# Thirty weight tiles get their rests from an accumulating load instead of a VectorE subtraction

## The chip, the cores and the metric

The kernel runs on one core of a Trainium2 chip. The metric is the device time of one execution in microseconds (us), from its start to its end. Lower is better.

## The reference

One layer of a hybrid streaming encoder runs on 512 prompt frames and 32 sample frames. The kernel holds both as T = 544 columns. Cut to what matters here:

```python
h = rmsnorm(x, p['norm_mix'])
proj = h @ p['w_in']
z, xbc, dt_raw, hq, hf, hi, hgate, rgate, rx, mg = jnp.split(proj, split_pts, axis=-1)
...  # three token mixers: Mamba-2 SSD -> y_mb, HGRN2 -> y_hg, RG-LRU -> y_rg
branches = jnp.stack([y_mb, y_hg, y_rg], axis=0)
pb = jnp.einsum('kblc,kcd->kbld', branches, p['w_branch'])
gates = jax.nn.sigmoid(mg.reshape(b, L, N_BRANCH, D_MODEL))
merged = jnp.einsum('kbld,blkd->bld', pb, gates)
x = x + merged @ p['w_out']
...  # SwiGLU FFN, final norm
```

HGRN2 uses four of these projections: hq (its query), hf (its forget gate), hi (its value) and hgate (its output gate), for eight heads of 128 channels each.

## The kernel before

**Tiles and products.** All weights lie in DRAM as 98 groups, one array per group of 128 partitions x 8 K-blocks x 256 columns (1024 KB; a few are smaller). A group gives two *tiles* of 128 output channels. One tile is one `Step`: its weights (128 x 1024 values per tile) against 544 columns of a right-hand side. The product of two float32 numbers is made of three products of rounded numbers (float32r): each weight w is split into a rounded half `wh` and the rest `wl` = w - wh, each right-hand side into hi and lo, and TensorE computes wh*hi, wh*lo and wl*hi. `products` (L321 ff., matmuls at L338) therefore issues 32 matmuls with `wh` and then 16 with `wl`, each of 128x272. HGRN2's heaviest projections (hq2, hi, hgt) run as `Pair` instead: two tiles in seven products of quarter size (matmuls at L347), whose weights `prep_pair` makes.

**The weights' two ways.** `load_raw` (L264, queue SP) brings a group to a `raw` buffer, of which there are two. `prep` makes `wh` and `wl` of one tile, for which there are three buffers each:

- the ordinary way: ScalarE copies the tile's columns to `wh` (L319), and VectorE subtracts, wl = raw - wh (L320). The tile's columns are 8 pieces of 128 in `raw`.
- the accumulating way, so far for `fi` groups only: ScalarE copies to `wh` (L314), ScalarE writes -wh to `wl` (L315), and GpSimd issues a DMA that reads the tile's weights again from DRAM and adds them to `wl` (L316). For this the group lies by tile in DRAM: a tile's 1024 values per partition are one piece. `lay_out` reorders those groups (named in `SEVEN`) on the host. `prep_pair` uses accumulating DMAs as well (L283, 512 KB; L286, 256 KB).

**What sets the order.** `run_program` walks a list of steps. Before a step's matmuls it emits the `prep` of the step after it and, as far as two raw buffers go, the loads. Between the matmuls of a step, `advance` runs pieces of *sides*: generators with the small work of the token mixers. A scheduler then orders each engine's instructions by priority and by its own estimate of when they are ready. On the chip, each engine executes its list in order and waits at an instruction whose semaphores are not there yet.

**The place of the change.** After the SSD phase come the early HGRN2 steps: four ordinary tiles (hq0, hq1), then nine pairs, whose results go to DRAM (`kept_hq`, `kept_hi`, `kept_hgt`, L1035 and L1044). Then the HGRN2 phase proper opens (`hg_open`, a new buffer pool) with this list, each name being two tiles unless a number of tiles stands beside it:

hf0, br0 (4 tiles), hf1, br0 (4 tiles), hf2, mg1 (2 tiles), hf3, hq3, mg1 (6 tiles), then br1 (8 tiles).

After each hf, `hg_heads` (L1089) loads q, v and gate of two heads from DRAM, and two sides `hg_side` begin: transposes of v (`tok_major`, L1117 to L1121), decays on VectorE (L1141 to L1219), small matmuls (L1159 to L1211), state and output (L1224 to L1264). In these, GpSimd clears and fills `at` (L1125, L1201) and takes the power -0.5 of the output's mean square (`oss`, L1254). Names in the profile: `acc` is a tile's PSUM accumulator, `mx` a PSUM buffer of a side, `hhi`/`hlo` and `yr` are right-hand sides, `gth` a gate, `hq` (a buffer's name) holds q, v or gate of a head, `qv` a head's scaled queries, `on` a head's normed output, `rs_mb` SSD norms, `kept_mg` gates kept in DRAM.

Of the kernel before, what the change touches and what calls it, by code (L numbers as in the profile page):

```python
# [49 lines left out]
B11, B21, B22, T1, T2, T3, T4 = range(7)  # L50

EARLY = ("hq2", "hi0", "hi1", "hi2", "hi3", "hgt0", "hgt1", "hgt2", "hgt3")
SEVEN = EARLY + tuple(f"fi{m}" for m in range(22))


# [41 lines left out]
WG = {k: (i, v[0][2] // P) for i, (k, v) in enumerate(GROUPS.items())}  # L97
# [23 lines left out]
def hybrid_layer(ctx: ExitStack, tc: _tile.TileContext, a: dict, outs: list):  # L121
# [146 lines left out]
    def quarters(t):  # L268
        return t.rearrange("p k n -> p (k n)").rearrange("p (q n) -> p q n", n=512)

    def prep_pair(st):

        r = quarters(raws[st.raw])
        src = wp[WG[st.raw][0]].rearrange("p (q n) -> p q n", n=512)
        tiles = []
        for i in range(4):
            pool = wpool if i % 2 else phase["p"]
            tiles.append([pool.tile([P, NK, P], R, tag=t, name=t, bufs=3) for t in ("wh", "wl")])
        (ah, al), (bh, bl), (dh, dl), (ch, cl) = [[t.rearrange("p (q k) n -> p q (k n)", q=2) for t in x] for x in tiles]
        sa, sc = ([pt_([P, 2, T], "sums", 3)[:, :, :512] for _ in range(2)])  # L280
        S.activation(bh, r[:, 0:2], AF.Copy)  # L281
        S.activation(bl, bh.bitcast(F), AF.Copy, scale=-1.0)  # L282
        G.dma_start(bl, src[:, 0:2], accum_op=ALU.add)  # L283
        S.activation(dh[:, 0], r[:, 3], AF.Copy)
        S.activation(dl[:, 0], dh[:, 0].bitcast(F), AF.Copy, scale=-1.0)  # L285
        G.dma_start(dl[:, 0], src[:, 3], accum_op=ALU.add)  # L286
        V.tensor_tensor(sa[:, 0], r[:, 0], r[:, 2], ALU.add)
        V.tensor_tensor(sa[:, 1], sa[:, 0], r[:, 3], ALU.add)
        S.activation(ah, sa, AF.Copy)
        V.tensor_tensor(sc[:, 0], r[:, 2], r[:, 3], ALU.add)  # L290
        V.tensor_tensor(sc[:, 1], sa[:, 1], r[:, 1], ALU.add)
        V.tensor_tensor(al, sa, ah.bitcast(F), ALU.subtract)  # L292
        S.activation(ch, sc, AF.Copy)  # L293
        V.tensor_tensor(cl, sc, ch.bitcast(F), ALU.subtract)
        q = lambda x, y, i: (x[:, i].rearrange("p (k n) -> p k n", n=P), y[:, i].rearrange("p (k n) -> p k n", n=P))
        st.wts = {"s3": q(ah, al, 0), "s2": q(ah, al, 1), "a11": q(bh, bl, 0), "a12": q(bh, bl, 1), "a22": q(dh, dl, 0),
                  "s1": q(ch, cl, 0), "s4": q(ch, cl, 1)}

    def prep(st):
        if isinstance(st, Pair):  # L300
            return prep_pair(st)
        if st.wh is not None:
            return
        if st.share:
            st.wh, st.wl = st.share.wh, st.share.wl
            return
        r = raws[st.raw]
        st.wh = wpool.tile([P, NK, P], R, tag="wh", name="wh")
        st.wl = wpool.tile([P, NK, P], R, tag="wl", name="wl")
        if st.raw.startswith("fi"):  # L310
            i = st.col // P
            src = quarters(r)[:, 2 * i : 2 * i + 2]
            wh, wl = (t.rearrange("p (a k) n -> p a (k n)", a=2) for t in (st.wh, st.wl))
            S.activation(wh, src, AF.Copy)  # L314
            S.activation(wl, wh.bitcast(F), AF.Copy, scale=-1.0)  # L315
            G.dma_start(wl, wp[WG[st.raw][0]].rearrange("p (q n) -> p q n", n=512)[:, 2 * i : 2 * i + 2], accum_op=ALU.add)  # L316
            return
        src = r[:, : st.nk, st.col : st.col + P]
        S.activation(st.wh[:, : st.nk, :], src, AF.Copy)  # L319
        V.tensor_tensor(st.wl[:, : st.nk, :], src, st.wh[:, : st.nk, :].bitcast(F), ALU.subtract)  # L320
# [60 lines left out]
    def run_program():  # L381
# [9 lines left out]
        for s in program:  # L391
            if not isinstance(s, (Step, Pair)):
                s()
                continue
            while prepped < min(len(order), done + 2):
                st = order[prepped]
                while loaded < min(len(keys), pos[st.raw] + RAWB):
                    if keys[loaded] not in raws:
                        load_raw(keys[loaded])
                    loaded += 1  # L400
                prep(st)
                prepped += 1
            if isinstance(s, Pair):
                pair_products(s)
            else:
                products(s)
            if isinstance(s, Step) and s.last and s.evac:
                with tc.high_priority(offset=400):
                    s.evac(accs[s.acc])
            done += 1  # L410
            advance(BUDGET[0] / TILE_PARTS)
# [135 lines left out]
    def head():  # L547
# [54 lines left out]
        square(NK - 1)  # L602
        st = Step("rg0", 0, NK, None, "rg0")
        prep(st)
        acc3 = [mx(), mx()]
        hd["rb"] = rb = pt_([P, T], "rbx")
# [18 lines left out]
        rg_gl[0] = g  # L625
        derived()
        prep(first[0])
        rg_load()

# [421 lines left out]
    program.append(drain)  # L1051
    for key in EARLY:
        kind, pr = key[:-1], int(key[-1])
# [287 lines left out]
    for m in range(8):  # L1341
        key = f"wo{m//2}"
# [228 lines left out]
def lay_out(v):  # L1571

    cm = lambda x: x.reshape(-1, P).T
    dcol = np.repeat(v["mb_d"][0], 64)
    rows = lambda x: np.broadcast_to(x.reshape(1, -1), (P, x.size))
    src = {
        "mcw": cm(v["mb_conv_w"]), "mcb": cm(v["mb_conv_b"]), "nw": cm(v["mb_norm_w"]), "ba": cm(v["rg_b_a"]), "bi": cm(v["rg_b_i"]),
        "hgw": cm(v["hg_norm_w"]), "nm": cm(v["norm_mix"]), "lb": cm(v["hg_lb_logits"]), "rcw": cm(v["rg_conv_w"]), "rcb": cm(v["rg_conv_b"]),
        "lam": cm(v["rg_lambda"]), "nf": cm(v["norm_ffn"]), "h0": cm(v["state_rglru"]), "rch": cm(v["state_rglru_conv"]),
        "sch": cm(v["state_ssm_conv"]), "dcol": cm(dcol), "dtb": rows(v["mb_dt_bias"]), "alog": rows(v["mb_a_log"]),  # L1580
    }
    mats = {"w_in": v["w_in"][0], "w_out": v["w_out"][0], "w_ffn_in": v["w_ffn_in"][0], "w_ffn_out": v["w_ffn_out"][0]}
    mats |= {f"w_branch{b}": v["w_branch"][0, b] for b in range(3)}
    weights = np.zeros((len(GROUPS), P, NK, 256), v["w_in"].dtype)
    for i, parts in enumerate(GROUPS.values()):
        c = 0
        for name, r0, nr, c0, ncol in parts:
            weights[i, :, : nr // P, c : c + ncol] = mats[name][r0 : r0 + nr, c0 : c0 + ncol].reshape(nr // P, P, ncol).transpose(1, 0, 2)
            c += ncol
    for key in SEVEN:  # L1590
        i = WG[key][0]
        weights[i] = weights[i].reshape(P, NK, 2, P).transpose(0, 2, 1, 3).reshape(P, NK, 256)
    gates = np.zeros((P, 2, 8, P), v["rg_w_a"].dtype)
    for i, name in enumerate(("rg_w_a", "rg_w_i")):
        w = v[name][0].reshape(8, 2, 64, 64).transpose(1, 2, 0, 3)
        gates[:64, i, :, :64] = w[0]
        gates[64:, i, :, 64:] = w[1]
    r = np.arange(P)[:, None]
    c = np.arange(P)[None, :]
    consts = [c == r, r <= c, r > c, r % 32 == c[:, :32], r % 16 == c[:, :16]]  # L1600
    for h in QUADS:
        for s in range(3):
            n = (3 - s) * h
            j = r % 32
            consts.append((j // (4 * h) == c[:, : 8 * (3 - s)] // n) & (j // h % 4 == s))
    consts.append(r % 32 // 16 == 0 * c[:, :16])
    return {
        "xT": np.concatenate([v["x_prompt"][0], v["x_sample"][0]], axis=0).T,
        "params": np.concatenate([src[k] for k in PK], axis=1),
        "consts": np.concatenate(consts, axis=1).astype(np.float32),  # L1610
        "weights": weights.reshape(len(GROUPS), P, NK * 256),
        "w_dt": v["w_in"][0][:, C_DT : C_DT + 16].reshape(NK, P, 16).transpose(1, 0, 2),
        "rg_gates": gates,
        "ssm_in": v["state_ssm"][0, 0].transpose(2, 0, 1).reshape(P, 1024),
        "hg_in": v["state_hgrn"][0, 0].transpose(1, 0, 2),
        "norm_final": rows(v["norm_final"]),
    }
# [23 lines left out]
```

## Time and profile before

| | |
|---|---|
| median of 3 runs (lowest to highest) | 1347.47 us (1345.01 to 1347.68) |
| the profiled execution's own time | 1345.73 us |
| its span, first to last instruction | 1344.0 us |
| TensorE busy (PE) | 1326.4 us |
| VectorE (DVE), ScalarE (ACT), GpSimd (POOL) busy | 864.3, 643.5, 162.4 us |
| mean clock granted to TensorE | 0.997 |

PE is TensorE's matmuls and PEld its weight loads; SP issues the plain DMAs and POOL the accumulating ones. A row such as "L338 PE ... xN | busy, mean | idle <-releaser" gives a group of instructions by source line and what ended the idle time before them. A window row gives, for a stretch of time, each engine's busy time with its count of instructions, the granted clock, the busy share of the 16 DMA engines and GB/s.

### The profile page before, as it was taken

Reading aid. Unit: us, or ns where it says so; the run is one execution under the profiler, and the core shown is the slowest. Engines: PE = TensorE matmul, PEld = TensorE weight load, DVE = VectorE, ACT = ScalarE, POOL = GpSimd, SP = SyncE. Lnnn points to the kernel's source line nnn. Section 1 sums busy time; section 2 is a strip of 40 time slices with the busy share of each in tenths; the row PEclk is TensorE's granted clock in tenths of the full one; section 3 lists DMA queues with packets and bytes.
Section 4 is the critical chain, followed back from the end, with each engine's and each line's share of the span. In section 5 each row is a group of like instructions: output and inputs, shape, how many; then the busy total and the mean of one; then the engine's idle time right before and its main releaser. Section 6 shows DMA issues by size and latency. Waiting matters only on the chain. (4 is left out here: it accounts for less than half of the span.)

```text
span 1344.0 us, 26318 instructions
## 1 busy us (share of the span) xinstructions
PE 1326.4 (99%) x11034; PEld 1274.2 (95%) x11034; DVE 864.3 (64%) x1617; ACT 643.5 (48%) x1063; POOL 162.4 (12%) x263
## 2 busy tenths in 40 slices
PE   9999999999999999999999999999999999999997
PEld 9999999999998999999998888999999999999997
DVE  8887653738575677656748766455597447744753
ACT  7785744236445346553324443334666236623634
POOL 3031001011020001110111121000111011101100
PEclk9999999999999999999999999999999999999998
DMA  6212121211222348875332032622767166725621
GB/s 238 95 63 95 64 99 65 102 66 64 75 74 76 112 120 221 223 178 190 117 131 102 25 125 85 217 95 97 186 160 168 66 172 152 168 75 167 142 77 68
DMA packets 43975, 161.73 MB, mean 120 GB/s; under 512 B 5040, under 2 KB 10032, under 8 KB 31824
## 3 DMA queue, kind: packets, MB, share of 16 engines
q1 hardware_dynamic: 34496, 134.35, 28.9%
q0 software_dynamic: 8928, 25.17, 10.8%
q8 instruction: 87, 1.43, 0.4%
q10 hardware_dynamic: 432, 0.53, 0.1%
q14 instruction: 32, 0.26, 0.1%
HBM read 145.04 MB, written 14.99 MB: 119 GB/s over the span
## 5 line engine op out<-in xcount | busy, mean ns | idle before, releaser
L319 ACT ACTIVATE wh<-raw 128x1024 fp32r<-128x1024 f32 (+1 forms) x132 | 137.8, 1045 | 256.4 <-PE acc L338 218.9
L338 PE MATMUL acc<-hhi,wh 128*128 128x272 f32 x1184 | 252.6, 293 | 0.4 <-ACT cv L463 0.4
L338 PE MATMUL acc<-hlo,wh 128*128 128x272 f32 x1184 | 249.7, 290 | 0.0
L320 DVE TENSOR_TENSOR wl<-raw,wh 128x1024 fp32r<-128x1024 f32 (+1 forms) x132 | 159.0, 1204 | 81.2 <-PE acc L338 68.9
L338 PE MATMUL acc<-yr,wh 128*128 128x272 f32 x1504 | 206.3, 290 | 0.5 <-DVE gth L497 0.4
L338 PEld LDWEIGHTS acc<-yr,wh 128*128 128x128 f32 x1504 | 194.3, 188 | 2.0 <-PE acc L338 0.6
L338 PEld LDWEIGHTS acc<-hhi,wh 128*128 128x128 f32 x1184 | 186.9, 189 | 4.2 <-issue 1.3
L338 PEld LDWEIGHTS acc<-hlo,wh 128*128 128x128 f32 x1184 | 186.0, 188 | 1.6 <-issue 0.2
L338 PE MATMUL acc<-hhi,wl 128*128 128x272 f32 x1184 | 167.7, 291 | 0.0
L338 PEld LDWEIGHTS acc<-hhi,wl 128*128 128x128 f32 x1184 | 154.6, 188 | 2.6 <-issue 0.9
L347 PE MATMUL acc<-T,wh 128*128 128x272 f32 x744 | 147.2, 290 | 0.2 <-DVE pt L376 0.2
L347 PEld LDWEIGHTS acc<-T,wh 128*128 128x128 f32 x744 | 113.5, 188 | 1.5 <-DVE pt L376 0.4
L338 PE MATMUL acc<-yr,wl 128*128 128x272 f32 x752 | 106.8, 289 | 0.0
L338 PEld LDWEIGHTS acc<-yr,wl 128*128 128x128 f32 x752 | 99.0, 188 | 0.3
L347 PE MATMUL acc<-T,wl 128*128 128x272 f32 x372 | 74.2, 288 | 0.0
L347 PE MATMUL acc<-Thhi,wh 128*128 128x272 f32 x304 | 63.5, 301 | 1.0 <-ACT pt L370 0.5
L347 PE MATMUL acc<-Thlo,wh 128*128 128x272 f32 x304 | 62.8, 288 | 0.0
L347 PE MATMUL acc<-Thhi,wl 128*128 128x272 f32 x304 | 60.2, 289 | 0.2 <-DVE wl L292 0.2
L347 PEld LDWEIGHTS acc<-T,wl 128*128 128x128 f32 x372 | 57.4, 188 | 0.0
L293 ACT ACTIVATE wh<-sums 128x1024 fp32r<-128x1024 f32 x28 | 29.7, 1061 | 53.7 <-PE acc L347 49.7
L286 POOL DMA_DIRECT2D wl<-in_weights_dram x28 | 24.8, 887 | 249.7 <-ACT wl L285 217.7
L347 PEld LDWEIGHTS acc<-Thhi,wh 128*128 128x128 f32 x304 | 45.8, 188 | 5.7 <-DVE pu L361 3.1
(440 smaller groups left out, 2285.0 us busy)
## 6 DMA issues: line engine op xcount, KB each, us to landing
raw<-in_weights_dram SPq DMA_DIRECT2D x93, 1024.0 KB, 4.8
wl<-in_weights_dram POOLq DMA_DIRECT2D x34, 512.0 KB, 7.1
wl<-in_weights_dram POOLq DMA_DIRECT2D x28, 256.0 KB, 3.8
kept_mg<-gth SPq DMA_DIRECT2D x16, 272.0 KB, 2.0
gth<-kept_mg SPq DMA_DIRECT2D x16, 272.0 KB, 5.6
raw<-in_weights_dram SPq DMA_DIRECT2D x4, 768.0 KB, 4.5
xt<-in_xT_dram SPq DMA_DIRECT2D x8, 272.0 KB, 5.5
kept_hi<-pt SPq DMA_DIRECT2D x8, 272.0 KB, 3.0
```

Source lines behind the costliest of these rows:

```text
L286: G.dma_start(dl[:, 0], src[:, 3], accum_op=ALU.add)
L293: S.activation(ch, sc, AF.Copy)
L319: S.activation(st.wh[:, : st.nk, :], src, AF.Copy)
L320: V.tensor_tensor(st.wl[:, : st.nk, :], src, st.wh[:, : st.nk, :].bitcast(F), ALU.subtract)
L338: PE.matmul(acc[:, h, :HALF], l, r[:, h * HALF : (h + 1) * HALF], start=st.first and i == 0, stop=st.last and i == len(seq) - 1)
L347: PE.matmul(out, w[:, kp, :], st.rhs(n == 1, kp, j), start=start and n == 0 and kp == 0, stop=stop and n == 2 and kp == 3, skip_group_chec ...
```

## The change

The ordinary tiles of the groups hf, hq, br0 and mg1 take the accumulating way. These are 8 + 6 + 8 + 8 = 30 tiles, in 15 groups; hq2, a pair, stays as it was. The 15 groups are laid out by tile in DRAM (hq2 already was). Nothing else is edited. Line numbers behind the edit are two higher in the changed kernel (L338 becomes L340).

```diff
 EARLY = ("hq2", "hi0", "hi1", "hi2", "hi3", "hgt0", "hgt1", "hgt2", "hgt3")
+
+ADDED = ("hf", "hq", "br0", "mg1")
 SEVEN = EARLY + tuple(f"fi{m}" for m in range(22))
@@ prep
-        if st.raw.startswith("fi"):
+        if st.raw in SEVEN or st.raw.startswith(ADDED):
             i = st.col // P
             src = quarters(r)[:, 2 * i : 2 * i + 2]
             wh, wl = (t.rearrange("p (a k) n -> p a (k n)", a=2) for t in (st.wh, st.wl))
@@ lay_out
-    for key in SEVEN:
-        i = WG[key][0]
+    for key, (i, _) in WG.items():
+        if key not in SEVEN and not key.startswith(ADDED):
+            continue
         weights[i] = weights[i].reshape(P, NK, 2, P).transpose(0, 2, 1, 3).reshape(P, NK, 256)
```

The scheduler orders the changed program anew. ScalarE's list at the opening of the HGRN2 phase, before; the four copies L319 are the `wh` of hf0's second tile and of br0's tiles 0, 1 and 2, L1067 takes hf0's results out of PSUM, and L1140 is the first head's first work on q:

```order
L319 ACTIVATE wh<-raw 128x1024
L370 ACTIVATE pt<-acc 128x272
L1042 ACTIVATE pt<-pt 128x544
L319 ACTIVATE wh<-raw 128x1024
L1041 ACTIVATE pt<-pt 128x272
L319 ACTIVATE wh<-raw 128x1024
L1067 ACTIVATE hth<-acc 128x544
L319 ACTIVATE wh<-raw 128x1024
L1067 ACTIVATE hth<-acc 128x544
L1140 ACTIVATE qv<-hq 128x136x4
```

And after the change (L316 is the `wh`, L317 the new -wh):

```order
L316 ACTIVATE wh<-raw 128x1024
L372 ACTIVATE pt<-acc 128x272
L317 ACTIVATE wl<-wh 128x1024
L1044 ACTIVATE pt<-pt 128x544
L316 ACTIVATE wh<-raw 128x1024
L1043 ACTIVATE pt<-pt 128x272
L317 ACTIVATE wl<-wh 128x1024
L316 ACTIVATE wh<-raw 128x1024
L1069 ACTIVATE hth<-acc 128x544
L317 ACTIVATE wl<-wh 128x1024
L316 ACTIVATE wh<-raw 128x1024
L1069 ACTIVATE hth<-acc 128x544
```

Each -wh stands behind the PSUM read (L1043, L1069) that came next after its `wh`.

GpSimd's list from hf0 on, after the change; before, it held none of the L318 (the accumulating loads of hf0 and br0's first tile, of br0's next three, and of hf1's first), and the rest in the same order:

```order
L318 DMA wl<-in_weights_dram 128x1024 x3
L1127 MEMSET at 128x512 x2
L318 DMA wl<-in_weights_dram 128x1024 x3
L1203 COPY at<-bd 32x4x32 x4
L318 DMA wl<-in_weights_dram 128x1024
```

The loads of br0's tiles 1 to 3 now stand between the clearing of `at` and the first head's copies into it.

TensorE's list at br0's first tile, where the first head's v is transposed for the first time, before:

```order
L338 MATMUL acc<-yr,wh 128x272 x32
L338 MATMUL acc<-yr,wl 128x272 x12
L1117 MATMUL mx_7025<-cst,hq 128x128 x4
L1120 MATMUL mx<-cst,hq 32x128
L1159 MATMUL mx<-qv,hth 32x80 x16
L1160 MATMUL mx<-qv,hth 32x80
L338 MATMUL acc<-yr,wl 128x272 x4
L1117 MATMUL mx_7160<-cst,hq 128x128 x4
```

And after:

```order
L340 MATMUL acc<-yr,wh 128x272 x32
L340 MATMUL acc<-yr,wl 128x272 x8
L1119 MATMUL mx_7033<-cst,hq 128x128 x4
L1122 MATMUL mx<-cst,hq 32x128
L1161 MATMUL mx<-qv,hth 32x80 x16
L1162 MATMUL mx<-qv,hth 32x80
L340 MATMUL acc<-yr,wl 128x272 x8
L1119 MATMUL mx_7168<-cst,hq 128x128 x4
```

The transposes have moved four matmuls of the tile forward.

TensorE's list between the fourth head's output matmuls (L1246) and the transposes of its normed output (L1262), before:

```order
L1246 MATMUL mx<-s_8159,hq 32x128
L1117 MATMUL mx_8652<-cst,hq 128x128 x2
L1120 MATMUL mx<-cst,hq 32x128
L338 MATMUL acc<-hhi,wh 128x272
L338 MATMUL acc<-hlo,wh 128x272 x2
L338 MATMUL acc<-hhi,wh 128x272 x2
L338 MATMUL acc<-hlo,wh 128x272 x2
L338 MATMUL acc<-hhi,wh 128x272 x2
L1159 MATMUL mx<-qv,hth 32x80 x16
L1160 MATMUL mx<-qv,hth 32x80
L338 MATMUL acc<-hlo,wh 128x272 x2
L1117 MATMUL mx_8782<-cst,hq 128x128 x4
```

And after, up to the same transposes (now L1264):

```order
L1248 MATMUL mx<-s_8177,hq 32x128
L1119 MATMUL mx_8673<-cst,hq 128x128 x4
L1122 MATMUL mx<-cst,hq 32x128
L340 MATMUL acc<-hhi,wh 128x272
L340 MATMUL acc<-hlo,wh 128x272 x2
L340 MATMUL acc<-hhi,wh 128x272 x2
L340 MATMUL acc<-hlo,wh 128x272 x2
L1119 MATMUL mx_8804<-cst,hq 128x128
L1161 MATMUL mx<-qv,hth 32x80 x16
L1162 MATMUL mx<-qv,hth 32x80
L1119 MATMUL mx_8804<-cst,hq 128x128 x3
L1264 MATMUL mx<-cst,on 128x128 x4
```

Of the tile's matmuls 7 now stand between the two, against 11, and 8 of the next heads' transposes against 6.

## Prediction

> **What bounds the kernel now.** The page's busy shares come first, then the window row of the stretch from hf0's first `wh` to the end of HGRN2 (columns: PE, PEld, DVE, ACT, POOL, clock, DMA share, GB/s), then TensorE's waits from 480 to 1000 us.
>
> ```profile
> span 1344.0 us, 26318 instructions
> PE 1326.4 (99%) x11034; PEld 1274.2 (95%) x11034; DVE 864.3 (64%) x1617; ACT 643.5 (48%) x1063; POOL 162.4 (12%) x263
> 597.00:864.00 267.00, 262.42 (x2781) 241.94 (x2780) 173.22 (x509) 95.76 (x230) 35.16 (x48) 1.00 0.34 119
> PE mx L1262 <- DVE on L1257: 2.1, 3, 1.1
> PE mx L1245 <- DVE on L1257: 1.4, 1, 1.4
> PE mx L1159 <- DVE qv L1148: 0.9, 4, 0.3
> ...
> PE acc L347 <- DVE pu L361: 0.4, 1, 0.4
> ...
> PE acc L347 <- DVE pt L376: 0.2, 1, 0.2
> ```
>
> TensorE is the bound. In the 267 us where 26 of the 30 tiles lie, VectorE is busy 65% of the time and ScalarE 36%, but TensorE idles 4.6 us. No row names the subtraction (L320) as what TensorE waited for. What the change can win is at most part of these 4.6 us and of 0.6 us in the early steps (pu and pt, the last two rows). What it can lose has no such limit, since it makes TensorE's operands depend on 30 more transfers.
>
> **The subtractions go.**
>
> ```profile
> 597.00:864.00 267.00, 36.70 (x30) 1.00 0.34 119
> L314 ACT ACTIVATE wh<-raw x6: 1046/1060/1065, 935.4 to 967.8; 128x1024 fp32r<-128x1024 f32 x6
> ...
> L315 ACT ACTIVATE wl<-wh x6: 1059/1060/1062, 937.5 to 969.8; 128x1024 fp32r<-128x1024 f32 x6
> ...
> L316 POOL DMA_DIRECT2D wl<-in_weights_dram x6: 862/862/936, 938.8 to 971.2; - x6
> DMA to landing us min/median/max: 5.3/5.5/6.2
> ...
> 751.58 0.69 DVE L1257 TENSOR_TENSOR on<-mx,oss 128x512 f32<-128x512 f32 x1 [1.28 <-POOL oss L1254]
> ...
> DMA to landing us min/median/max: 5.3/7.4/10.9
> ```
>
> The first row is L320 alone in the stretch: 1.22 us each, so VectorE loses 30 x 1.22 = 36.7 us. Of TensorE's waits only those on L1148 (0.9) and on the early pt and pu (0.2 and 0.4) can be VectorE's load; the ends are 0 and -1.5. L1257 waits idle for GpSimd's power (row of 751.58), not behind other VectorE work, so its 3.5 us stay. I take -0.3, nearer to 0, because the order of TensorE's list moves with VectorE's.
>
> **The new work, by tile.** ScalarE gets 30 x 1.06 = 31.8 us and GpSimd 30 x 0.86 = 25.9 us. Both have room; the wait for the third `wl` buffer and the landing count:
>
> ```profile
> 674.79 1.06 ACT L319 ACTIVATE wh<-raw 128x1024 fp32r<-128x1024 f32 x1 [2.48 <-PE acc L338]
> 680.87 1.06 ACT L319 ACTIVATE wh<-raw 128x1024 fp32r<-128x1024 f32 x1 [5.01 <-PE acc L338]
> ...
> 480.00:500.00 20.00, 20.00 (x160) 19.79 (x159) 15.72 (x25) 11.49 (x16) 3.12 (x3) 1.00 0.45 154
> 700.00:760.00 60.00, 57.16 (x706) 50.35 (x706) 46.04 (x155) 25.07 (x69) 9.71 (x14) 1.00 0.24 81
> ```
>
> Tiles without side work follow each other every 6.0 us. `wh` starts when the tile three before is through its 32 first matmuls, 4.0 us into it. Its `wl` buffer is free at 6.0, -wh is there at 7.1, and the load, 10.9 us at the slowest landing seen (the pairs' 512 KB loads, last row of the fence before), is there at 18.0. TensorE needs it at 3 x 6.0 + 4.0 = 22.0. Cover: 4 us, so nothing; where sides lengthen a tile, more. The four early tiles (hq0, hq1) follow each other without sides' work too, between 484 and 509 us, where the transfer engines are 45% and VectorE 79% busy: the same cover, 0. If the cover were gone, TensorE would stand at the 33rd matmul of each tile. Behind -wh on ScalarE stand PSUM reads and side copies, at most 1.1 us later each; the order lists put -wh behind the PSUM read that frees the accumulator. On GpSimd, the power of a head may wait behind one issue of 0.86 us; where -wh was ready before, as for hf3 and hq3 ahead of the third and fourth heads, it waits for nothing. Nothing taken for either, between 0 and +0.9 per head. The raw buffers come free without the subtraction, about 1.2 us earlier; loads were not waited for here, so 0. By-tile layout: L314 and L319 last 1.06 us alike, 0.
>
> **The transfers, and the first two heads.** This is the term that decides. Page rows of the two queues; then, from the DMA answers, a raw load with no accumulating load near it (issued at 607 us), two that ran beside a pair's two accumulating loads (in the windows 541 to 552 and 552 to 563), and the first head's v; then the window 618 to 624.
>
> ```profile
> q1 hardware_dynamic: 34496, 134.35, 28.9%
> q0 software_dynamic: 8928, 25.17, 10.8%
> ...
> raw<-in_weights_dram SPq DMA_DIRECT2D x1, 1024.0 KB, 5.2
> ...
> raw<-in_weights_dram SPq DMA_DIRECT2D x1, 1024.0 KB, 6.5
> ...
> raw<-in_weights_dram SPq DMA_DIRECT2D x1, 1024.0 KB, 8.9
> ...
> hq<-kept_hi SPq DMA_DIRECT2D x1, 272.0 KB, 7.0
> ...
> 618.00:624.00 6.00, 6.00 (x51) 6.00 (x50) 2.93 (x5) 1.69 (x2) 0.00 (x0) 1.00 0.97 331
> ```
>
> 10.8% of 1344 us for 25.17 MB makes 5.8 us per MB on all 16 engines, against 2.9 for plain loads: a tile's accumulating load of 512 KB takes 3.0 us of them, as much as a whole raw load. Between 618 and 624 us the engines are already 97% busy. What is in flight there, and who waits:
>
> ```profile
> 612.58 1.06 ACT L319 ACTIVATE wh<-raw 128x1024 fp32r<-128x1024 f32 x1 [2.28 <-PE acc L338]
> 615.47 0.63 ACT L1067 ACTIVATE hth<-acc 128x544 f32<-128x544 f32 x1 [1.83 <-DMA kept_hgt<-pt]
> 615.57 0.99 POOL L1125 MEMSET at<- 128x512 f32 x2 [25.87 <-DMA kept_hgt<-pt]
> 617.33 0.43 SPq L264 DMA_DIRECT2D raw<-in_weights_dram  x1
> 618.75 1.38 SPq L1089 DMA_DIRECT2D hq<-kept_hi  x2
> 620.35 4.18 PE L338 MATMUL acc<-yr,wh 128*128 128x272 f32 x32
> 624.37 1.67 PE L338 MATMUL acc<-yr,wl 128*128 128x272 f32 x12
> 625.87 0.60 PE L1117 MATMUL mx<-cst,hq 128*128 128x128 f32 x4
> L1117 PEldq EVENT_SEMAPHORE  x5: 51/51/1806, 623.6 to 626.9; - x5
> ```
>
> The new pool opens when the last kept_hgt lands (615.5). Then SP issues gates, a raw load (617.3), q, v and gate of two heads, in this order. v of the first head is issued at 618.75 and TensorE transposes it at 625.87. The last row says that there was no slack: TensorE's weight queue waited 1.8 us at L1117, by my reading from 623.6 to 625.4. After the change, br0's tile 1 has its -wh behind L1067, from 616.1 to 617.2; its load goes out behind the two clearings at about 617.2, so beside the raw load and the heads'. br0's tile 2 follows at about 622.3 (-wh behind the L1067 at 620.5).
>
> How much later v comes: at least by its share of the bytes, 512 KB at q1's 2.9 us per MB, 1.5 us; at most by the first accumulating load's 3.0 us and a half-share of the second's until v is in, 1.8, together 4.8, and 1.0 more if the kept_hgt stores also land later beside the loads of hf0 and br0's first tile. The raw loads beside 768 KB of accumulating loads took 1.3 to 3.7 us longer. I take 3.5, between one whole load (3.0) and the worst row, since 618 to 624 is as full as those stretches. In the new order TensorE arrives after 40 instead of 44 matmuls, at 624.37 + 8 x 0.126 = 625.4, just when v used to come. So it stands 3.5 us (1.5 to 5.8). The first q, +3.5 as well, goes through ScalarE and VectorE while v is transposed, so it is not counted twice. The Trainium skill, "DMA: Bandwidth & Descriptors", section "Queues, rings and completion order", says that a DMA engine takes turns between queues packet by packet; by it the plain queue goes at about half speed while the other has work, and the loss here would be the 3.0 to 4.8 us above; the raw rows agree.
>
> The next heads' loads also meet accumulating loads:
>
> ```profile
> 667.39 1.26 SPq L1089 DMA_DIRECT2D hq<-kept_hi  x2
> 699.59 0.58 ACT L1118 COPY vtok<-mx 128x512 f32<-128x512 f32 x1
> ```
>
> Their v is issued at 667.4 and its transposes are copied out at 699.6, 32 us later: 0.
>
> **The order of TensorE's list.**
>
> ```profile
> 747.61 0.41 PE L1246 MATMUL mx<-s,hq 128*32 128x128 f32 x2
> 750.73 0.60 PE L1117 MATMUL mx<-cst,hq 128*128 128x128 f32 x4
> 752.42 0.63 PE L1262 MATMUL mx<-cst,on 128*128 128x128 f32 x4 [1.08 <-DVE on L1257]
> ```
>
> The fourth head's chain (squares, power, `on`) takes 4.4 us from L1246's end, and TensorE has work for less. The new order takes 4 matmuls out, 4 x 0.126 = 0.5, and puts 2 transposes of 0.15 in: +0.2. At the fifth head two matmuls fewer stand there: +0.25, in a wait of 0.6.
>
> **Sum.** -0.3 + 3.5 + 0.2 + 0.25 = +3.65 us. On the profiled execution, 1345.73 + 3.65 = 1349.4. The median of the runs shown lies 1.74 above that execution, which is the scatter of three runs; I set the sum on the middle of the two, 1346.6, and forecast 1350.2.
>
> **Rivals.** All on 1346.6. *Cheap sharing, no change:* v comes only 1.5 us later because accumulating loads cost their bytes; then +1.65, 1348.3. For it speaks the raw row of 6.5; against it, 8.9 and the queue shares. Here the Trainium skill speaks against my price: the same page, section "Anatomy of one DMA — SWDGE (gpsimd) path", fits a DMA issued by GpSimd as 2.0 us plus bytes / 436e3, an estimate of 1.2 us of data for 512 KB; that would give a sum of about +1.4, where the rows of L316 say 5.3 at best with nothing beside it, not 3.2. *Faster:* VectorE, 46 of 60 us busy from 700 to 760 in places without a gap, was behind the stalls; with 36.7 us less, L1148's 0.9, L1262's 2.1 and the early 0.6 close, and v comes in time: -3.6, 1343.0. It decides only if both hold and more than 2.7 us close. Against it stands GpSimd's power ahead of L1257. *Much slower:* GpSimd's list in order: four powers wait behind loads whose -wh waits for TensorE's release, 2 us each: +8, 1354.6. 16 matmuls of 0.126 are those 2 us. It decides if such a -wh stands ahead of the power when the squares are done; the cover above and the earlier -wh speak against it.
>
> **How the numbers follow.** A measurement of this kernel tells about 0.2%, 2.7 us, from no change. Chances: forecast 0.50 (its own range +2 to +6), cheap sharing 0.31, faster 0.10, much slower 0.09. A quarter of the forecast's case falls under 2.7 us. Slower is then 0.375 + 0.09, same 0.31 + 0.125, faster 0.10. The range goes from 1345.0, which leaves out the faster case, to 1354.5.
>
> **What would show it.** TensorE's wait at the first L1119 (v's transposes, about 625 us) of 1.5 to 6 us, with the first heads' loads landing 9 to 11 us after issue instead of 7; L322 on VectorE 30 fewer; no wait of L340 on a `wl` load; waits on `on` about 3.9 us as before. Wrong, if L1119 starts by 626 us, if the waits on `on` grow by more than 2 us, or if `wl` loads stop TensorE.

## The result, and the profile after

| | before | after |
|---|---|---|
| median of 4 runs each (lowest to highest) | 1346.89 us (1345.01 to 1347.68) | 1355.42 us (1353.62 to 1356.46) |
| ratio, 95% interval | | 1.0069 [1.0057, 1.0081] |
| profiled span | 1344.0 us | 1354.6 us |

The change costs 8.5 us. The prediction had the sign and the place; its 1350.2 us was 5.2 too low, and its range (to 1354.5) did not reach the result. The page of the changed kernel (engines, then the two DMA queues: packets, MB, share of the span), and then the window from hf0's first `wh` to the end of HGRN2, which was 267 us long before:

```profile
span 1354.6 us, 26391 instructions
PE 1326.6 (98%) x11034; PEld 1274.8 (94%) x11034; DVE 831.7 (61%) x1587; ACT 671.5 (50%) x1093; POOL 183.8 (14%) x293
q1 hardware_dynamic: 34496, 134.35, 29.0%
q0 software_dynamic: 13248, 40.90, 17.3%
```

```profile
597.00:874.00 277.00, 262.64 (x2773) 242.17 (x2771) 144.98 (x483) 119.65 (x256) 53.27 (x74) 0.98 0.61 164
```

VectorE lost its 30 instructions and 32.6 us, ScalarE gained 28 us, GpSimd 21. TensorE does the same work (1326.6 against 1326.4 us), in a window that is 10 us longer and at a granted clock of 0.98 in place of 1.00. TensorE's waits from 480 to 1000 us say where:

```profile
PE mx L1119 <- DMA hq<-kept_hq: 10.1, 1, 10.1
PE mx L1264 <- DVE on L1259: 1.5, 2, 1.1
PE mx L1247 <- DVE on L1259: 1.3, 1, 1.3
PE mx L1161 <- DVE qv L1150: 0.6, 3, 0.2
...
PE acc L349 <- DMA wl<-in_weights_dram: 0.3, 1, 0.3
```

One wait of 10 us is new: the first head's transposes of v. (`hq` is a buffer's name; the profile names the group of loads by its first, v's is `kept_hi`.) All others are within 0.3 us as they were, or shorter, and no accumulating load stops its own tile. The opening in the timeline of the changed kernel (start, duration, then idle time before and what ended it):

```profile
606.94 2.41 SPq L1046 DMA_DIRECT2D kept_hgt<-pt  x2
610.24 0.86 POOL L318 DMA_DIRECT2D wl<-in_weights_dram  x1 [3.01 <-ACT wl L317]
618.18 0.62 ACT L1069 ACTIVATE hth<-acc 128x544 f32<-128x544 f32 x1 [5.63 <-DMA kept_hgt<-pt]
620.04 0.86 POOL L318 DMA_DIRECT2D wl<-in_weights_dram  x1 [0.78 <-ACT wl L317]
621.81 1.27 SPq L1091 DMA_DIRECT2D hq<-kept_hi  x2
622.45 0.86 POOL L318 DMA_DIRECT2D wl<-in_weights_dram  x1 [1.54 <-ACT wl L317]
634.55 1.08 PE L1119 MATMUL mx<-cst,hq 128*128 128x128 f32 x4 [10.05 <-DMA hq<-kept_hq]
639.05 0.60 PE L1119 MATMUL mx<-cst,hq 128*128 128x128 f32 x4
```

And the transfers (KB each, us from issue to landing): the `kept_hgt` stores before and after, then after alone the raw load ahead of v, and v:

```profile
kept_hgt<-pt SPq DMA_DIRECT2D x2, 272.0 KB, 4.3
```
```profile
kept_hgt<-pt SPq DMA_DIRECT2D x1, 272.0 KB, 8.5
raw<-in_weights_dram SPq DMA_DIRECT2D x1, 1024.0 KB, 9.0
hq<-kept_hi SPq DMA_DIRECT2D x2, 272.0 KB, 12.7
```

The ten microseconds are made of three pieces. The stores take 4.2 us longer from issue to landing, beside the accumulating loads of hf0's second and br0's first tile. The first store was issued earlier (606.94 instead of 610.32), but the new pool opens at 618.2 instead of 615.5, although TensorE itself was 1.0 us ahead (hf0's first tile ended at 613.3 instead of 614.3): 3.7. Then v takes 12.7 us from issue to landing in place of 7.0, beside the accumulating loads of 620.04 and 622.45: 5.7. And TensorE arrives 4 matmuls earlier than in the old order: 0.5. Together 9.9.

The fourth loss is no wait at all. Windows of TensorE alone (stretch, busy time and count, granted clock, DMA share, GB/s):

```profile
624.00:628.00 4.00, 0.50 (x5) 1.00 1.00 249
628.00:634.00 6.00, 0.00 (x0) 0.55 1.04 287
634.00:639.00 5.00, 4.45 (x47) 0.52 0.83 318
639.00:645.00 6.00, 6.00 (x109) 1.00 0.57 116
```

TensorE idles from 624.5; from 628.6 to 638.8 it is granted half its clock. Four transposes take 1.08 us at 634.55, and four like them 0.60 at 639.05. Work from 634.55 to 638.8 at half speed costs 2.1 us more.

### The profile page after: what moved, and what is told of

The parts are those of the page before. It is cut to its first block, busy times and chain, and to the rows that moved or that the text cites. A ratio compares the mean times of both kernels' runs of the same rounds, so it can differ in the third digit from the quotient of the medians.

```text
span 1354.6 us, 26391 instructions
## 1 busy us (share of the span) xinstructions
PE 1326.6 (98%) x11034; PEld 1274.8 (94%) x11034; DVE 831.7 (61%) x1587; ACT 671.5 (50%) x1093; POOL 183.8 (14%) x293
## 5 line engine op out<-in xcount | busy, mean ns | idle before, releaser
L340 PE MATMUL acc<-hhi,wh 128*128 128x272 f32 x1184 | 253.4, 293 | 0.4 <-ACT cv L465 0.4
L340 PE MATMUL acc<-hlo,wh 128*128 128x272 f32 x1184 | 248.0, 290 | 0.0
L340 PE MATMUL acc<-yr,wh 128*128 128x272 f32 x1504 | 206.2, 290 | 0.5 <-DVE gth L499 0.4
L321 ACT ACTIVATE wh<-raw 128x1024 fp32r<-128x1024 f32 (+1 forms) x102 | 106.0, 1041 | 196.3 <-PE acc L340 164.1
L340 PEld LDWEIGHTS acc<-yr,wh 128*128 128x128 f32 x1504 | 194.3, 188 | 1.9 <-PE acc L340 0.6
L340 PEld LDWEIGHTS acc<-hhi,wh 128*128 128x128 f32 x1184 | 187.1, 189 | 4.4 <-issue 1.3
L340 PEld LDWEIGHTS acc<-hlo,wh 128*128 128x128 f32 x1184 | 186.0, 188 | 1.1 <-issue 0.2
L340 PE MATMUL acc<-hhi,wl 128*128 128x272 f32 x1184 | 167.2, 291 | 0.0
L322 DVE TENSOR_TENSOR wl<-raw,wh 128x1024 fp32r<-128x1024 f32 (+1 forms) x102 | 122.2, 1198 | 67.8 <-PE acc L340 61.0
L340 PEld LDWEIGHTS acc<-hhi,wl 128*128 128x128 f32 x1184 | 154.5, 188 | 2.3 <-issue 0.9
L340 PE MATMUL acc<-yr,wl 128*128 128x272 f32 x752 | 108.1, 291 | 0.0
L340 PEld LDWEIGHTS acc<-yr,wl 128*128 128x128 f32 x752 | 99.7, 190 | 0.7 <-issue 0.2
L318 POOL DMA_DIRECT2D wl<-in_weights_dram x36 | 31.8, 883 | 288.0 <-ACT wl L317 271.2
L316 ACT ACTIVATE wh<-raw 128x1024 fp32r<-128x1024 f32 x36 | 38.1, 1058 | 58.0 <-PE acc L340 52.8
L288 POOL DMA_DIRECT2D wl<-in_weights_dram x28 | 24.2, 864 | 251.3 <-ACT wl L287 215.4
```

The source lines that it names most:

```text
L340: PE.matmul(acc[:, h, :HALF], l, r[:, h * HALF : (h + 1) * HALF], start=st.first and i == 0, stop=st.last and i == len(seq) - 1)
```

## The experiments

**The six opening tiles back to the subtraction.** hf0's two tiles and br0's first four, 24 of the 30 left:

```diff
-ADDED = ("hf", "hq", "br0", "mg1")
+ADDED = ("hf1", "hf2", "hf3", "hq", "br0_2", "br0_3", "mg1")
```

> The six tiles at the opening (hf0's two, br0's first four) get their rests by the subtraction again; the other 24 ordinary tiles keep the accumulating loads. Theory A (the accumulating loads in flight between 604 and 632 us delay first the kept_hgt stores, and so the new pool, and then the first head's v): TensorE's wait at L1119 under 1 us, the kept_hgt stores landing in 4 to 5 us, v in 7 to 8 us after issue, clock 1.00 in that stretch; time 1344 to 1348, as the kernel before. Rival B (order: the work added on ScalarE and GpSimd at the opening delays the issue, bytes don't matter): the same here, told apart by later runs. Rival C (small costs spread over all 30 tiles, of which the opening is only the most visible): +6 to +7 of the +8.5 us stay.

Measured: 1344.12 us against 1345.99 for the kernel before, ratio 0.9983 [0.9974, 0.9993]. Pool and v are back, and there is no wait at L1119 (timeline):

```profile
614.85 0.62 ACT L1069 ACTIVATE hth<-acc 128x544 f32<-128x544 f32 x1 [1.52 <-DMA kept_hgt<-pt]
625.56 0.60 PE L1119 MATMUL mx<-cst,hq 128*128 128x128 f32 x4
```

That is theory A's number, and rival C falls: the other 24 tiles cost nothing, they win 1.9 us. This is a version that beats both kernels, by a little.

**The converse: only those six tiles accumulate** (`ADDED = ("hf0", "br0_0", "br0_1")`).

> The converse: only the six tiles at the opening take the accumulating load, the other 24 the subtraction. Theory A: wait at L1119 of 9 to 11 us, a granted clock of 0.6 to 0.8 just behind it, time +8 to +10 on the kernel before. Rival C: about +2, 6/30 of the loss.

Measured: 1358.03 us against 1345.99, ratio 1.0078 [1.0057, 1.0098]. TensorE stands 8.0 us at L1119, with a low clock until 640.4, and 1.1 us more than before (0.2) at a pair's `wl`. The timeline's row, and one of TensorE's waits:

```profile
635.08 1.08 PE L1119 MATMUL mx<-cst,hq 128*128 128x128 f32 x4 [7.99 <-DMA hq<-kept_hq]
```

```profile
PE acc L349 <- DMA wl<-in_weights_dram: 1.3, 2, 0.9
```

The wait is 1 us shorter than theory A had it, the time 2 us longer (+12.0). The whole loss is there without the 24 tiles, and without their 1.9 us of gain. The wait of 8.0, half of the 5.3 us from its end to the clock's return, and the `wl` wait's 1.1 make 11.8, as much as its span grew (1355.8 against 1344.0).

**hf0 alone back** (`ADDED = ("hf1", "hf2", "hf3", "hq", "br0", "mg1")`).

> Only hf0's two tiles go back to the subtraction; br0's tiles still accumulate, so that two accumulating loads fewer are in flight while the kept_hgt stores run, and as many as in the changed kernel beside the raw load and the first head's. Theory A: the pool opens 3 to 4 us earlier, v still comes 4 to 5 us later after its issue; wait at L1119 about 6 us, time +4 to +6. Rival B: if the delay of the opening came from GpSimd's or ScalarE's list, the stores land as late as with the change (8.5 us) and the wait stays at 9 to 10.

Measured: 1352.17 us against 1345.99, ratio 1.0042 [1.0031, 1.0052]; pool and TensorE in the timeline, v's landing, and the window behind the wait:

```profile
615.34 0.62 ACT L1069 ACTIVATE hth<-acc 128x544 f32<-128x544 f32 x1 [1.69 <-DMA kept_hgt<-pt]
631.33 1.08 PE L1119 MATMUL mx<-cst,hq 128*128 128x128 f32 x4 [5.73 <-issue]
```

```profile
hq<-kept_hi SPq DMA_DIRECT2D x1, 272.0 KB, 11.9
```

```profile
630.00:637.00 7.00, 5.67 (x52) 0.53 0.58 233
```

The profile names nothing that ended this wait ("issue"), but it is v: issued at 619.38 and 11.9 us on its way, v is there at 631.3. The two rows with "issue" in the next runs are read in the same way. The pool opens as before the change; v still comes 4.9 us later after its issue, and TensorE waits 5.7. Time +6.2 instead of the expected 4 to 6: the slow clock, which the expectation had left out.

**br0's first four tiles alone back** (`ADDED = ("hf", "hq", "br0_2", "br0_3", "mg1")`).

> Only br0's first four tiles go back to the subtraction; hf0's two accumulate. Theory A: nothing accumulates beside the first head's loads, so v lands in about 7 us; hf0's loads still delay the stores by 1 to 3 us; wait at L1119 2 to 4 us, time +1 to +3. Rival B (hf0's work in the lists alone decides): wait near 10.

Measured: 1345.94 us against 1345.99, ratio 0.9998 [0.9988, 1.0008]; pool and TensorE in the timeline, v's landing, and the window of the wait:

```profile
615.97 0.62 ACT L1069 ACTIVATE hth<-acc 128x544 f32<-128x544 f32 x1 [2.96 <-DMA kept_hgt<-pt]
627.44 0.63 PE L1119 MATMUL mx<-cst,hq 128*128 128x128 f32 x4 [1.97 <-issue]
```

```profile
hq<-kept_hi SPq DMA_DIRECT2D x2, 272.0 KB, 7.4
```

```profile
625.00:628.00 3.00, 1.03 (x9) 1.00 0.75 284
```

v lands in 7.4 us, the wait is 2.0, and the clock stays whole. Wait and gain cancel, 1 us under what was expected. So v's delay belongs to br0's loads. The opening's is less clear: in these profiled executions the pool opens at 616.0 with hf0's loads alone and at 615.3 with br0's alone, against 615.5 before and 618.2 with both (617.0 in a second execution, below). That is one execution each, and among the ten of this kernel one took 1349.6 us at a mean clock of 0.995.

**The same lists, but the six loads overwrite instead of adding.** The instructions of every engine stand in the same order as in the changed kernel, so only the kind of transfer differs (`wp[...]...` stands for the tile's weights in DRAM; the sum with -wh is left out, so these `wl` are not the rests):

```diff
-G.dma_start(wl, wp[...]..., accum_op=ALU.add)
+G.dma_start(wl, wp[...]..., **({} if st.raw.startswith(OPEN) else {"accum_op": ALU.add}))   # OPEN = hf0, br0_0, br0_1
```

> Every engine's list as in the changed kernel, but the loads into the `wl` of the six opening tiles overwrite instead of adding (so that these rests are wrong): the same bytes from GpSimd at the same places. Theory A1 (an accumulating load occupies the transfer engines for 3.0 us per 512 KB, twice a copy's 1.5): the kept_hgt stores land in about 6 us instead of 8.5, v about 9.5 us after its issue instead of 12.7; wait at L1119 4 to 6 us, time +2 to +4 on the kernel before. Theory A2 (the bytes and the second queue count, not the adding): wait 9 to 10, time +8. Rival B (places in the lists): wait 10, since the lists are the same.

Measured: 1349.99 us against 1345.64, ratio 1.0027 [1.0014, 1.0040]. v's landing, its transposes in the timeline, and the software queue from 617 to 629 us; then the software queue in the changed kernel from 620 to 635, and there both queues from 626 to 632, while both have work (packets, MB, share of 16 engines):

```profile
hq<-kept_hi SPq DMA_DIRECT2D x2, 272.0 KB, 10.3
```

```profile
628.58 1.09 PE L1119 MATMUL mx<-cst,hq 128*128 128x128 f32 x4 [3.75 <-issue]
```

```profile
q0 software_dynamic: 288, 1.05, 23.9%
```
```profile
q0 software_dynamic: 288, 1.05, 35.8%
```
```profile
q0 software_dynamic: 243, 0.93, 78.3%
q1 hardware_dynamic: 243, 0.52, 26.1%
```

Two loads' 1.05 MB take 0.239 x 12 = 2.9 us of all engines as copies and 0.358 x 15 = 5.4 us when they add. v lands in 10.3 us instead of 12.7, and the wait falls from 10 us (7.3 in a second execution, below) to 3.75. That is A1: the adding itself is dear. The last two rows show what it does to the neighbour: both queues move the same 243 packets, but the adding ones take three times as long for 1.8 times the bytes, so that the plain queue has a quarter of the engines' time. Time is 0.3 above A1's window; the clock was low from 626.9 to 633.8, which no theory had in it. The loss is not steady: four of the ten executions took 1345.8 to 1347.0 us at a mean clock of 0.998, the other six, the profiled one among them, 1349.6 to 1352.7 us at 0.995 to 0.997.

**The same lists, a quarter of the columns** (`wl[:, :, :128]` and its source, for the six loads).

> The same lists again, the six opening loads add, but only a quarter of the columns (128 of each 512; the other rests are wrong): a quarter of the bytes in as many descriptors' rows of a quarter's length. Theory A: the delays shrink with the bytes, kept_hgt landing about 5.4 us, v about 8.5 after issue, wait at L1119 1 to 3.5 us, no lower clock, time -1 to +2 on the kernel before. Rival B (places in the lists): the wait stays at 10 us.

Measured: 1346.00 us against 1345.64, ratio 1.0005 [0.9996, 1.0015]; v's landing, and its transposes in the timeline:

```profile
hq<-kept_hi SPq DMA_DIRECT2D x2, 272.0 KB, 7.7
```

```profile
626.54 0.63 PE L1119 MATMUL mx<-cst,hq 128*128 128x128 f32 x4 [1.35 <-DMA hq<-kept_hq]
```

With -wh, issues and lists all in place, the wait is 1.35 us, and the clock stays whole. Rival B falls: places in ScalarE's and GpSimd's lists cost at most that.

**The whole change, with v's transposes later.**

```diff
         kts = pt_([TS, P], "kts", 2)
+        if h == 0: yield 17.0
```

> The whole change, and the first head's side work is held back behind its first loads, so that v's transposes stand about 104 matmuls (13 us) later in TensorE's list. If the loss is only that TensorE arrives 10 us before v: no wait at L1119, clock 1.00, and a time of 1343 to 1346, as with the six opening tiles left out. If small costs of the 30 loads remain, or the later start of the heads' chain costs elsewhere (the heads' `on` waits, the tiles behind HGRN2), 1347 to 1352.

Measured: 1350.77 us against 1345.64, ratio 1.0042 [1.0027, 1.0057]. A miss; from the timeline:

```profile
634.19 0.54 DVE L1143 TENSOR_TENSOR qv<-hq,hgg 128x272 f32<-128x272 f32 x1 [10.94 <-DMA hq<-kept_hq]
636.63 0.71 DVE L499 SCALAR_TENSOR_TENSOR gth<-gth,acc 128x544 f32<-128x544 f32 x1
637.40 6.29 PE L340 MATMUL acc<-yr,wh 128*128 128x272 f32 x32 [4.21 <-DVE gth L499]
```

TensorE no longer waits at L1119. But VectorE stands 10.9 us at the first work on q, from the same batch of loads, and behind it in its list is the read that frees br0's accumulators. TensorE waits 4.2 us for those, and the clock falls again (635.1 to 641.9). Moving one consumer of a late load only moves the stall to the next.

**br0's tiles 2 and 3 back** (`ADDED = ("hf", "hq", "br0_0", "br0_2", "br0_3", "mg1")`): one accumulating load beside v instead of two.

> br0's tiles 2 and 3 go back to the subtraction: one accumulating load (tile 2's, issued 0.6 us after v's own issue) fewer beside the first head's loads; everything up to the new pool's opening as with the change. By the prediction's half share of it, 1.8 us: v about 11 us after issue, wait about 8. If a load issued behind v still holds it up for its whole 3.0 us: v 9.5 to 10 us after issue, wait 6 to 7. Time +4 to +6.5.

Measured: 1352.78 us against 1345.64, ratio 1.0052 [1.0037, 1.0067]; its v and its transposes:

```profile
hq<-kept_hi SPq DMA_DIRECT2D x2, 272.0 KB, 11.1
```

```profile
631.37 1.09 PE L1119 MATMUL mx<-cst,hq 128*128 128x128 f32 x4 [4.98 <-DMA hq<-kept_hq]
```

v lands in 11.1 us, the time (+7.1) is above the window. The second load thus costs v about 1.6 us, near the prediction's half share of 1.8. The first costs 4.1 on the 7.0 of before, more than its 3.0 us of engine time, and that excess isn't explained. But the wait was 5.0, not 8. In this kernel's list the transposes stand four matmuls later, as before the change (0.5), and the pool opened 8.5 us after the first store's issue (616.8 less 608.3), with the same transfers in flight up to then as in the changed kernel, where it took 11.3. So both kernels were profiled a second time.

**The changed kernel again, and the kernel just above again.**

> The changed kernel once more, for a second profiled execution of the opening. In the first the new pool opened 11.3 us after the first kept_hgt store's issue (618.3 to 606.9); in the kernel with only the six opening tiles changed and in the one with br0's tiles 2 and 3 plain, where the same transfers were in flight, 8.5 and 8.6. If the lists fix it: 11 us again. If it is scatter of the transfers from execution to execution: anything from 8.5 to 11.3, and the wait at L1119 smaller by as much.

> The kernel with br0's tiles 2 and 3 plain once more, for a second look: v landing about 11 us after its issue again (one accumulating load beside it) if the load and not chance sets it; the pool's opening 8.5 to 11.3 us after the stores' issue.

Measured, single executions: 1354.46 and 1354.11 us, beside 1345.13 for the kernel before, all on another chip than the experiments above. The stores, the pool and the transposes in the timeline and v's landing, first of the changed kernel, then of the other:

```profile
608.31 2.42 SPq L1046 DMA_DIRECT2D kept_hgt<-pt  x2
617.13 0.99 POOL L1127 MEMSET at<- 128x512 f32 x2 [4.64 <-DMA kept_hgt<-pt]
633.20 1.09 PE L1119 MATMUL mx<-cst,hq 128*128 128x128 f32 x4 [7.32 <-DMA hq<-kept_hq]
```

```profile
hq<-kept_hi SPq DMA_DIRECT2D x2, 272.0 KB, 12.8
```
```profile
607.59 2.41 SPq L1046 DMA_DIRECT2D kept_hgt<-pt  x2
619.17 0.99 POOL L1127 MEMSET at<- 128x512 f32 x2 [7.41 <-DMA kept_hgt<-pt]
632.86 1.09 PE L1119 MATMUL mx<-cst,hq 128*128 128x128 f32 x4 [7.20 <-DMA hq<-kept_hq]
```

```profile
hq<-kept_hi SPq DMA_DIRECT2D x2, 272.0 KB, 10.4
```

Now the changed kernel opens after 8.8 us and the other after 11.6. So the opening's delay is scatter between two values, 8.5 to 8.8 and 11.3 to 11.6, and both values come with either kernel and on either chip: it is not a matter of the lists. v's 12.7 and 12.8 with two loads, 11.1 and 10.4 with one, are the loads'. Of the first profile's 10.05 us, some 2.7 were this scatter.

**Does it add up?** Span of the profiled execution less 1344.0, against the wait of the opening, plus half of the time from the restart to the clock's return, less the 2.0 us that the 24 tiles' span wins:

| kernel | wait | slow clock | sum less 2.0 | span |
|---|---|---|---|---|
| the change | 10.05 | (638.8 - 634.55) / 2 = 2.1 | +10.2 | +10.6 |
| the change again | 7.3 | (637.3 - 633.2) / 2 = 2.1 | +7.4 | +8.5 |
| hf0 back | 5.7 | (637.4 - 631.3) / 2 = 3.0 | +6.7 | +7.2 |
| br0's four back | 2.0 | 0 | 0.0 | -0.2 |
| copies | 3.75 | (633.8 - 628.6) / 2 = 2.6 | +4.3 | +4.5 |
| a quarter | 1.35 | 0 | -0.7 | 0.0 |
| v's transposes later | 4.2 | (641.9 - 637.4) / 2 = 2.3 | +4.5 | +5.8 |
| br0's 2 and 3 back | 5.0 | (637.0 - 631.4) / 2 = 2.8 | +5.8 | +6.7 |
| br0's 2 and 3 back, again | 7.2 | (638.8 - 632.9) / 2 = 3.0 | +8.2 | +8.3 |

Up to 1.3 us of a span stay unplaced, and about 0.4 of the change's own. (The 1.3 are those with v's transposes later, where a tile also waits 0.5 us for its own accumulating load.)

## Why the prediction was wrong in size

- **Place, mechanism and sign: right.** The one new wait is the one named, at the first L1119, from loads that land late; no L340 waits for a `wl` load; waits on `on` did not grow (2.8 us against 3.5; the prediction's "about 3.9 us as before" has its +0.45 in it); GpSimd's list and the raw buffers cost nothing.
- **v's later landing, put at 3.5 (at least 1.5, at most 4.8): 5.7.** The step that failed is how much of the two loads was charged to v: a middle was taken, and even the upper end, one load whole and the second by half, was too low. The price of one load was right: 3.0 us predicted, 5.4 / 2 = 2.7 measured in that stretch. But v stands behind the gates, the raw load and q of its batch, and both loads were through before it landed (the software queue moves no packet after 633.5, v lands at 634.5): their 5.4 us of engine time are near its 5.7. The match is not exact, since one load alone cost v 3.4 to 4.1. The Trainium skill, "DMA: Bandwidth & Descriptors", section "Queues, rings and completion order", has the engines take turns between queues packet by packet, which the prediction cited beside its upper figures of 3.0 to 4.8. The rows agree in the turns, 243 packets against 243. They do not bear out the half speed that the prediction drew from it: the plain queue had 26.1% of the engines' time, the other 78.3%.
- **The `kept_hgt` stores, put at 1.0 at most and only in the upper bound: 3.7 in the profiled execution, about 1.0 in the second, whose wait was 2.7 shorter.** The same two-load reckoning should have been made for them, since two accumulating loads were in flight there as well. I priced the batch that I had in view and left the one ahead of it to the margin. With 3.0 us per load, two of them against a landing of 4.3 was a term of the sum.
- **The arrival of TensorE, put at just when v used to come: 0.5 early.** v used to land at 625.75 (618.75 + 7.0), the new order brings TensorE there at about 625.4.
- **The clock, not in the sum at all: 2.1.** A wait of several us was forecast, and nothing was added for its aftermath. The trace of before could not show it in this stretch, whose clock row is 1.00 throughout. The Trainium skill, "TensorE: Matmul & The Clock Gate", section "Part 1: The HAM clock gate", states it: half rate after an idle window of about 3.4 us, full rate after a busy one. By that rule the forecast wait of 3.5 us already stood at the edge, and it was a term that I left out.
- **VectorE's relief, put at -0.3: about -1.9,** by the kernel with 24 tiles (its interval is -0.9 to -3.5 us). TensorE's idle time did not fall there (span less busy time, 17.7 us against 17.6); what shrank is its busy time for the same instructions, 1324.3 us against 1326.4. Why wasn't tried, so the cause of this gain stays open.
- **The fourth and fifth head's order, +0.45:** not seen.
- **The rivals.** Cheap sharing (v 1.5 later) and GpSimd's list are excluded by rows. The "faster" rival had about half of its size right (1.9 us of 3.6, without the opening's loads), but not its mechanism, since the stalls that it wanted to close did not close.

So +3.65 became, for the profiled execution, 3.65 + 2.2 (v) + 3.7 (stores) + 0.5 (arrival) + 2.1 (clock) - 1.6 (relief) - 0.45 (order) = +10.1, where its span grew by 10.6. With the stores' shorter value it is +7.4; the medians' +8.5 lies between.

## What to carry to other kernels

Before a transfer is made dearer or added, list every batch that is in flight with it and ask of each what waits for its last member; a load at the end of a batch pays for all that was issued around it. Apply such a change where nothing in flight is needed soon: here 24 tiles won 1.9 us, and six at a phase's opening lost 12. Full transfer engines alone were no loss. In the kernel with the 24 tiles they are 95% busy from 665 to 690 us, against 49% before, and TensorE does not idle there:

```profile
665.00:690.00 25.00, 25.00 (x202) 1.00 0.95 261
```

Where a wait of TensorE of 3.75 us or more is forecast, add 2 to 3 us for the clock that comes back later; waits of up to 2.0 us cost none here, and between the two nothing was measured.

## What was not expected of the hardware

- **The clock.** Waits of 1.35 and 2.0 us left the clock whole; 3.75, 4.2, 5.0, 5.7, 7.2, 7.3, 8.0 and 10.05 us each halved it. It stayed half for 6.8 us in five executions (630.6 to 637.4 with hf0 back), where work resumed 0.8 to 2.6 us after the fall, and for 10.2 us in three (628.6 to 638.8 with the change), where it resumed after 4.3 to 6.0 us. The Trainium skill, "TensorE: Matmul & The Clock Gate", section "Part 1: The HAM clock gate", gives free-running windows of 3.413 us; two or three of those are 6.8 and 10.2, so the traces agree. With the copies it fell 2.1 us after TensorE's last matmul, so by such windows the one that counted as idle was not idle from end to end.
- **Adding costs about twice a copy in engine time:** 5.4 us against 2.9 for the same 1.05 MB from the same queue, at the same place in the lists. The plain queue beside it had a quarter of the engines' time here, not half.
- **Two values for the same stores:** with the same transfers around them the last store landed 8.5 to 8.8 or 11.3 to 11.6 us after the first one's issue. The executions whose first store was issued earlier (606.9 to 607.8) had the longer value, those from 608.3 on the shorter. In the last 1.5 us before the pool opens the 16 engines are 5 to 11% busy in the three longer ones, about as much as one engine or two, and 98% or more in the three shorter ones. So in the longer ones the last packets of the stores trail behind all other work, on few engines. Why stays open.
